# Where the output gates' weights are written, whose room the third merge gate takes, and where two splits stand on ScalarE

## The chip, the core and the metric

The kernel runs on one core of a Trainium2 chip. The core has several engines, each with a queue of its own that it works through in order: PE (TensorE, matrix products), ACT (ScalarE), DVE (VectorE), POOL (GpSimd) and SP (SyncE, which here issues most DMAs). They wait for each other through semaphores. The metric is the device time of one execution in microseconds (us). Three runs of the kernel before took 936.44, 936.89 and 935.8 us, a median of 936.44.

## What is computed

One layer of a hybrid decoder in float32, over 512 positions with 16 meta tokens ahead of them and a model width of 1024. A forgetting-attention branch and an mLSTM branch share the normalised input; two sigmoid gates merge them.

```
h = rms_norm(x, g_pre);  z = h @ w_in
(fq, fk, fv, ff, fz, mqk, mv, mi, mf, mo, mz, ga, gb) = jnp.split(z, SPLIT_POINTS, axis=-1)

oa = forgetting_attention(fq, fk, fv, log_sigmoid(ff + b_fox_f))      # 8 heads of 128, causal, blocks of 128
ya = (oa * jax.nn.silu(fz)) @ w_a

qk = jax.nn.silu(causal_conv(mqk, conv_w, conv_b));  mq, mk = jnp.split(qk, 2, axis=-1)
hb = mlstm_scan(mq, mk, mv, mi + b_i, log_sigmoid(mf + b_f))          # 4 heads, chunks of 128
hb = jax.nn.sigmoid(mo) * hb
hb = rms_norm(hb, g_head)                                             # per head
yb = (hb * jax.nn.silu(mz)) @ w_b

merged = jax.nn.sigmoid(ga) * ya + jax.nn.sigmoid(gb) * yb
return x + rms_norm(merged @ w_o, g_post)
```

`mo` is the output gate of the mLSTM heads, `mz` its silu gate, `ga` and `gb` are the merge gates, `fq` the queries of the attention.

## The kernel before

**Arithmetic.** Every float32 operand of a product is split in two: a high part in the type fp32r (a copy by ACT, name ending in `_h`) and the remainder (a subtraction by DVE, name ending in `_l`). One product is then three matmuls (`mm3`, L149 to L152). Weights arrive raw by DMA (`_r`), are split, and then read by PE.

**Seven products instead of eight.** Most projections multiply 2x2 blocks by the scheme of Strassen and Winograd. `st_products` runs seven block products in the order X, Y, Z, W, Y, X, Z. Some results must be kept aside in between, in a tile called `snap`: ACT copies it after the second product (L318), after the fourth (L323) and after the sixth (L328), and DVE joins the parts at the end (L331, L332, L334). The copy of L318 must be over before PE may write the fifth product into the same bank. The weights of the products are letters: `a` (a11), then sums. `st_narrow` (256 columns) makes a, b, c, d; `st_wide` (512 columns) makes a to g. Its sums are DVE additions in the raw tiles (L281, L282, L287, L289 in `st_wide`; L261, L262, L267, L268 in `st_narrow`), each followed by splits.

**Stages.** For each of four mLSTM heads h: convolution, values, scores (`score_part`: products, times decay L766, split L767, L769, and for the meta tokens L771), output gate (`mo_part`, wide, weights `wo{h}`, banks `po`, snap `so`), values times scores (`value_part`, banks `pna`, `pnb`), silu gates (`mz_part`, narrow, weights `wz{h}0`, `wz{h}1`). In the tile names an index of the head stands behind the letters: wo1c is letter c of head 1's output gate, wz10b letter b of its first silu unit. After the heads come attention queries (`fq_part`, snap `fqs`), keys (`fk_part`), merge gates (`ga_part`, `gb_part`, through `gate_part`, snap and result `sga`, `sgb`), the attention itself (probabilities `pth`, `ptl`, products `pfo`), and at the end the output products `pya`, `pout`. `ga_part` stores its result to DRAM (`d_sa`, L982, on ACT's DMA queue).

**What sets the order.** A scheduler orders the instructions of each engine by the order in which the program writes them and by what they depend on. Tiles are taken from pools under a tag; a new tile of a tag waits until the old one's last reader is done. The raw weights rotate through four rooms, so do `whi` and `wlo`; the tags `w` (decay weights of the scores, then `so`, later `fqs`), `sg` (merge gates) and `big_l` (remainders of transposed rows or probabilities) have one room each. Where the program wants an order without a dependency it uses `behind(x, y)` (L369): x is put behind y in the schedule, with no semaphore.

## Time and profile before

| | |
|---|---|
| median of three runs | 936.44 us |
| profiled execution | 936.34 us |
| its span, first to last instruction | 934.5 us |
| mean granted TensorE clock | 0.996 |

The time between the span and the execution, 1.8 us, lies outside the instructions. Rows of the profile read so: in a timeline, start in us, duration, engine, line, operation, output <- inputs, shape, and in brackets how long the engine had been idle and what ended that. In a view of waits: engine, tile and line that waited, `<-` what it waited for, then total us, number of waits and the longest. In a windows row: the stretch, its length, then for each engine its busy time and instructions, the clock, the DMA share and GB/s.

### The profile page before, as it was taken

The numbers are of one execution on the slowest core, as the hardware profiler recorded it, in microseconds if no ns is written. First come the engines' busy times: TensorE is split into PE (matmuls) and PEld (weight loads), VectorE is DVE, ScalarE is ACT, GpSimd is POOL, SyncE is SP. The second block draws the span as 40 slices with busy tenths as digits, with TensorE's granted clock in tenths as the row PEclk, the third lists the DMA queues.
The fourth block names the chain that finished last, engine by engine and source line by source line (L and its number), as shares of the span: only waits on it lengthen the run. The fifth ranks groups of instructions, "written<-read, shape, count | busy, mean of one in ns | idle before, by whom it ended". The sixth has DMA issues, their size and how long they took to land. (4 is left out here: it accounts for less than half of the span.)

```text
span 934.5 us, 16333 instructions
## 1 busy us (share of the span) xinstructions
PE 909.3 (97%) x6568; PEld 854.5 (91%) x6568; DVE 709.9 (76%) x1168; ACT 491.3 (53%) x840; POOL 110.0 (12%) x168
## 2 busy tenths in 40 slices
PE   8999999999999999999999999999999999999997
PEld 6998899899998999989899979899998999998887
DVE  6889688589787698876988856588885687995534
ACT  5646556546565455663565425455763554863231
POOL 3052000100101000010000002121331121300000
PEclk9999999999999999999999999999999999999999
DMA  7213143123331333232233344224352224358402
GB/s 231 93 49 102 46 134 93 34 68 94 122 103 57 90 91 92 97 96 72 71 114 92 101 125 138 73 75 136 95 190 75 75 69 137 97 190 306 136 23 91
DMA packets 76614, 97.51 MB, mean 104 GB/s; under 512 B 5237, under 2 KB 62677, under 8 KB 76538
## 3 DMA queue, kind: packets, MB, share of 16 engines
q1 hardware_dynamic: 74472, 92.76, 32.3%
q0 software_dynamic: 576, 2.10, 0.6%
q10 hardware_dynamic: 1490, 1.61, 0.5%
q8 instruction: 51, 0.84, 0.4%
q14 instruction: 25, 0.20, 0.1%
HBM read 90.62 MB, written 5.83 MB: 103 GB/s over the span
## 5 line engine op out<-in xcount | busy, mean ns | idle before, releaser
L151 PE MATMUL pyb<-bl,wb_h 128*128 128x512 f32 x128 | 49.9, 389 | 0.0
L152 PE MATMUL pyb<-bh,wb_l 128*128 128x512 f32 x128 | 49.8, 389 | 0.0
L150 PE MATMUL pyb<-bh,wb_h 128*128 128x512 f32 x128 | 49.8, 389 | 0.0
L1019 POOL TENSOR_SCALAR pn<-lt,rsum 128x128 f32<-128x128 f32 x32 | 29.3, 917 | 131.5 <-DVE rsum L1017 96.0
L733 DVE SCALAR_TENSOR_TENSOR y<-z,gc,y 128x512 f32<-128x512 f32 (+1 forms) x48 | 36.0, 756 | 2.1 <-ACT y L726 1.4
L150 PE MATMUL pfk<-hh,wfk_h 128*128 128x264 f32 x128 | 36.4, 285 | 0.0
L150 PE MATMUL pqk<-hh,wq_h 128*128 128x258 f32 x128 | 36.4, 284 | 0.0
L150 PE MATMUL pqk<-hh,wk_h 128*128 128x264 f32 x128 | 36.3, 284 | 0.0
L151 PE MATMUL pfk<-hl,wfk_h 128*128 128x264 f32 x128 | 36.3, 284 | 0.0
L152 PE MATMUL pqk<-hh,wk_l 128*128 128x264 f32 x128 | 36.3, 284 | 0.0
L152 PE MATMUL pfk<-hh,wfk_l 128*128 128x264 f32 x128 | 36.3, 283 | 0.0
L151 PE MATMUL pqk<-hl,wk_h 128*128 128x264 f32 x128 | 36.3, 283 | 0.0
L152 PE MATMUL pqk<-hh,wq_l 128*128 128x258 f32 x128 | 36.1, 282 | 0.0
L151 PE MATMUL pqk<-hl,wq_h 128*128 128x258 f32 x128 | 36.0, 282 | 0.0
L849 POOL TENSOR_TENSOR mrs<-mss,mhalf 128x1 f32<-128x1 f32 x16 | 12.2, 760 | 195.4 <-DVE r L836 157.1
L152 PEld LDWEIGHTS pyb<-bh,wb_l 128*128 128x128 f32 x128 | 24.0, 188 | 4.9
L151 PEld LDWEIGHTS pyb<-bl,wb_h 128*128 128x128 f32 x128 | 24.0, 188 | 4.9
L150 PEld LDWEIGHTS pyb<-bh,wb_h 128*128 128x128 f32 x128 | 24.0, 188 | 4.9
L144 DVE TENSOR_TENSOR wo_l<-wo_r,wo_h 128x1024 fp32r<-128x1024 f32 x12 | 15.7, 1314 | 16.9 <-ACT wo_h L142 16.9
L1016 ACT ACTIVATE lt<-lt,mn 128x144 f32<-128x144 f32 (+3 forms) x32 | 18.3, 572 | 17.9 <-DVE mn L1011 17.9
L884 DVE TENSOR_TENSOR yb<-pyb,yb 128x512 f32<-128x512 f32 x24 | 16.5, 687 | 14.2 <-PE pyb L152 14.2
L142 ACT ACTIVATE wo_h<-wo_r 128x1024 fp32r<-128x1024 f32 x12 | 12.7, 1059 | 24.4 <-PE pya L151 13.2
(2062 smaller groups left out, 3870.5 us busy)
## 6 DMA issues: line engine op xcount, KB each, us to landing
wv_r<-in_w_in_dram SPq DMA_DIRECT2D x16, 512.0 KB, 4.1
wo_r<-in_w_in_dram SPq DMA_DIRECT2D x16, 512.0 KB, 3.7
wz_r<-in_w_in_dram SPq DMA_DIRECT2D x16, 512.0 KB, 3.8
wb_r<-in_w_b_dram SPq DMA_DIRECT2D x16, 512.0 KB, 3.6
ab<-d_na SPq DMA_DIRECT2D x8, 672.0 KB, 3.9
wq_r<-in_w_in_dram SPq DMA_DIRECT2D x8, 512.0 KB, 3.8
wk_r<-in_w_in_dram SPq DMA_DIRECT2D x8, 512.0 KB, 4.4
wfq_r<-in_w_in_dram SPq DMA_DIRECT2D x8, 512.0 KB, 3.8
```

Of the source, the lines that this page charges most:

```text
L142: pin(S.activation(hi, raw, AF.Copy))
L144: pin(V.tensor_tensor(lo, raw, f(hi), ALU.subtract))
L150: T.matmul(ps, ah, bh, start=start, stop=False, **kw)
L151: T.matmul(ps, ah, bl, start=False, stop=False, **kw)
L152: T.matmul(ps, al, bh, start=False, stop=stop, **kw)
L733: V.scalar_tensor_tensor(y[:, t0:L], z[:, m, t0 + j:L + j], gc[:, j * 16 + mi:j * 16 + mi + 1], y[:, t0:L], ALU.mult, ALU.add)
L849: G.tensor_tensor(rs, ss, mhalf, ALU.pow)
L884: V.tensor_tensor(dst, ps[i], dst, ALU.add)
L1016: S.activation(lt[:, 0:kn], lt[:, 0:kn], AF.Exp, bias=mn[:, li:li + 1], scale=-1.0, accum_out=rsum)
L1019: G.tensor_scalar(pn[:, o:o + P].rearrange("p (g t) -> p g t", g=4), lt[:, 0:32].unsqueeze(1).to_broadcast([P, 4, 32]), rsum, None, ALU.mult)
```

## The change

Four edits; the work is the same, only its order and one room differ.

1. For heads 1 to 3 the output gate's `st_wide` (its loads, sums and splits) is written ahead of `score_part`, and its result passed to `mo_part`.
2. In `fq_part(0)` the last sum and the last split of the weights are put behind the last additions and the last sigmoid of the silu gate before (`mz_part.late`).
3. In `gb_part(0)` the first split is put behind the last snap copy of `ga_part(0)`.
4. `ga_part(2)` takes the room `big_l` of the pool `wk` instead of `sg`.

```diff
@@ -253,11 +253,13 @@
         split.first = first
         return hi, lo
 
-    def st_narrow(c0, name, into=None, late=None):
+    def st_narrow(c0, name, into=None, late=None, first=None):
 
         (r0,), (r1,) = (wload(win, 512 * i, 4, c0, 256, f"{name}{i}")[0] for i in range(2))
         a, b = slice(0, P), slice(P, 2 * P)
         o = {"a11": split(r0[:, :, a], f"{name}a", ("whs", "wls"), mw, 1, into)}
+        if first:
+            behind(split.first, first)
         V.tensor_tensor(r0[:, :, a], r0[:, :, a], r0[:, :, b], ALU.add)
         V.tensor_tensor(r0[:, :, b], r0[:, :, b], r1[:, :, b], ALU.add)
         x, y = split(r0, f"{name}b")
@@ -325,7 +327,7 @@
         between(1)
         prod("X", "s2", "t2")
         for wz, yx, snap, _ in units:
-            S.activation(snap[:, 2], yx[:, 256:512], AF.Copy)
+            st_products.copied = S.activation(snap[:, 2], yx[:, 256:512], AF.Copy)
         prod("Z", "s4", "b22")
         for wz, yx, snap, _ in units:
             V.tensor_tensor(yx[:, 256:512], snap[:, 0], yx[:, 256:512], ALU.subtract)
@@ -780,13 +782,13 @@
             S.activation(so[:, b, :], pn[b], AF.Sigmoid)
         return so
 
-    def mo_part(h):
+    def mo_part(h, w):
         so = sb([P, NCH, MV], F32, "w", f"so{h}")
         pn = banks(f"po{h}", NCH)
 
         snaps = [so.rearrange("p s (m n) -> p m s n", m=2)[:, m] for m in range(2)]
         units = [(pn[m], pn[2 + m], snaps[m], slice(m * P, m * P + P)) for m in range(2)]
-        added = st_products(st_wide(C_MO + h * MV, f"wo{h}"), units)
+        added = st_products(w, units)
 
         dry = line(wk, f"dry{h}", 1, tag="ss", bufs=8)
         pin(S.activation(dry, mhalf, AF.Sigmoid))
@@ -797,10 +799,11 @@
         mo_part.late = late
         return so
 
-    def st_unit(c0, name, room, into=None, late=None):
+    def st_unit(c0, name, room, into=None, late=None, first=None):
 
         ps = banks(f"p{name}", 2)
-        st_products(st_narrow(c0, f"w{name}", into, late), [(ps[0], ps[1], room.rearrange("p a (b n) -> p (a b) n", b=2), None)])
+        st_unit.added = st_products(st_narrow(c0, f"w{name}", into, late, first),
+                                    [(ps[0], ps[1], room.rearrange("p a (b n) -> p (a b) n", b=2), None)])
         return ps
 
     def mz_part(h, u):
@@ -811,7 +814,7 @@
             into = t[:, 0], t[:, 1]
         ps = st_unit(C_MZ + h * MV + u * 256, f"z{h}{u}", g, into, mo_part.late if h and not u else None)
         for m in range(2):
-            S.activation(g[:, m, :], ps[m], AF.Sigmoid)
+            mz_part.late = st_unit.added, S.activation(g[:, m, :], ps[m], AF.Sigmoid)
         for m in range(2):
             mi = 80 + h * 4 + u * 2 + m
             V.scalar_tensor_tensor(g[:, m, :], ps[m], gc[:, mi:mi + 1], g[:, m, :], ALU.mult, ALU.mult)
@@ -912,8 +915,9 @@
             next(tokens, None)
             wpk = score_part(h, q, k, w)
         else:
+            wo_ = st_wide(C_MO + h * MV, f"wo{h}")
             wpk = score_part(h, q, k, w)
-            so = mo_part(h)
+            so = mo_part(h, wo_)
         hts, gz = [None] * NCH, []
         value_part(h, wpk, v, so, hts, (3, 2))
         gz.append(mz_part(h, 0))
@@ -923,7 +927,8 @@
 
 
     def fq_part(p):
-        ps = st_unit(C_FQ + p * 256, f"fq{p}", sb([P, 2, SEQ], F32, "w", f"fqs{p}"))
+        ps = st_unit(C_FQ + p * 256, f"fq{p}", sb([P, 2, SEQ], F32, "w", f"fqs{p}"),
+                     late=None if p else mz_part.late)
         s = -(FD ** -0.5)
         qh = sb([P, 2, SEQ], F32R, "qk0h", f"fqh{p}")
         ql = sb([P, 2, SEQ], F32R, "qk0l", f"fql{p}")
@@ -964,22 +969,23 @@
             S.activation(sz[:, m, :], ps[m], AF.Sigmoid)
             V.tensor_tensor(sz[:, m, :], ps[m], sz[:, m, :], ALU.mult)
 
-    def gate_part(c0, u, name):
-        sg = sb([P, 2, SEQ], F32, "sg", f"s{name}{u}", gp)
-        ps = st_unit(c0 + u * 256, f"{name}{u}", sg)
+    def gate_part(c0, u, name, first=None, room=("sg", gp)):
+        sg = sb([P, 2, SEQ], F32, room[0], f"s{name}{u}", room[1])
+        ps = st_unit(c0 + u * 256, f"{name}{u}", sg, first=first)
         for m in range(2):
             S.activation(sg[:, m, :], ps[m], AF.Sigmoid)
         return sg
 
     def gb_part(u):
 
-        sg = gate_part(C_GB, u, "gb")
+        sg = gate_part(C_GB, u, "gb", None if u else ga_part.copied)
         y = yb[:, 2 * u:2 * u + 2, :]
         G.tensor_tensor(y, y, sg, ALU.mult)
         nc.gpsimd.dma_start(d_yb[u], y)
 
     def ga_part(u):
-        nc.scalar.dma_start(d_sa[u], gate_part(C_GA, u, "ga"))
+        nc.scalar.dma_start(d_sa[u], gate_part(C_GA, u, "ga", room=("big_l", wk) if u == 2 else ("sg", gp)))
+        ga_part.copied = st_products.copied
 
     def prob_part(p, m, q, k):
 
```

All line numbers from the second edit on shift, by 2 in most of what follows (L318 becomes L320, L328 becomes L330, L766 becomes L768, L771 becomes L773), and by 5 or 6 near the end.

The first place is DVE in head 1, from the decay of the scores on (`w`, `wl`, `wh`: score weights; `wo1b_l` and so on: remainders of the output gate's weights). Before:

```order
L769 TENSOR_TENSOR wl_2310<-w_1874,wh_2309 128x512
L769 TENSOR_TENSOR wl_2310<-w_1874,wh_2309 128x384
L769 TENSOR_TENSOR wl_2310<-w_1874,wh_2309 128x256
L766 TENSOR_TENSOR w_1874<-ps_2341,w_1874 128x128
L766 TENSOR_TENSOR w_1874<-ps_2351,w_1874 128x512
L769 TENSOR_TENSOR wl_2310<-w_1874,wh_2309 128x128
L282 TENSOR_TENSOR wo_r_2368<-wo_r_2368,wo_r_2372 128x1024
L771 TENSOR_TENSOR wh_2309<-w_1874,wh_2309 32x512
L252 TENSOR_TENSOR wo1b_l<-wo_r_2366,wo1b_h 128x1024
L252 TENSOR_TENSOR wo1c_l<-wo_r_2368,wo1c_h 128x1024
L252 TENSOR_TENSOR wo1d_l<-wo_r_2370,wo1d_h 128x1024
L252 TENSOR_TENSOR wo1e_l<-wo_r_2372,wo1e_h 128x1024
```

After, from the second sum on:

```order
L284 TENSOR_TENSOR wo_r_2306<-wo_r_2306,wo_r_2310 128x1024
L252 TENSOR_TENSOR wo1b_l<-wo_r_2304,wo1b_h 128x1024
L768 TENSOR_TENSOR w_1874<-ps_2351,w_1874 128x512
L252 TENSOR_TENSOR wo1c_l<-wo_r_2306,wo1c_h 128x1024
L252 TENSOR_TENSOR wo1d_l<-wo_r_2308,wo1d_h 128x1024
L771 TENSOR_TENSOR wl_2350<-w_1874,wh_2349 128x512
L768 TENSOR_TENSOR w_1874<-ps_2361,w_1874 128x384
L252 TENSOR_TENSOR wo1e_l<-wo_r_2310,wo1e_h 128x1024
L771 TENSOR_TENSOR wl_2350<-w_1874,wh_2349 128x384
L289 TENSOR_TENSOR wo_r_2310<-wo_r_2304,wo_r_2310 128x1024
L768 TENSOR_TENSOR w_1874<-ps_2371,w_1874 128x256
L291 TENSOR_TENSOR wo_r_2308<-wo_r_2308,wo_r_2310 128x1024
```

and right behind these:

```order
L252 TENSOR_TENSOR wo1f_l<-wo_r_2310,wo1f_h 128x1024
L771 TENSOR_TENSOR wl_2350<-w_1874,wh_2349 128x256
L252 TENSOR_TENSOR wo1g_l<-wo_r_2308,wo1g_h 128x1024
L768 TENSOR_TENSOR w_1874<-ps_2381,w_1874 128x128
L768 TENSOR_TENSOR w_1874<-ps_2391,w_1874 128x512
L771 TENSOR_TENSOR wl_2350<-w_1874,wh_2349 128x128
L252 TENSOR_TENSOR wz10a_l<-wz_r_2672,wz10a_h 128x512
L773 TENSOR_TENSOR wh_2349<-w_1874,wh_2349 32x512
```

Sum L282 (now L284) and the remainders b, c, d have moved ahead of most of the score weights; the last of these, L771 (now L773), has moved from ahead of b to behind g. On ACT at the same place the splits c to g, the copies of `so` and the first silu weights stood so before:

```order
L250 ACTIVATE wo1c_h<-wo_r_2368 128x1024
L250 ACTIVATE wo1d_h<-wo_r_2370 128x1024
L250 ACTIVATE wo1e_h<-wo_r_2372 128x1024
L318 ACTIVATE so_2361<-po_2_2364 128x2x256
L318 ACTIVATE so_2361<-po_3_2365 128x2x256
L250 ACTIVATE wz10a_h<-wz_r_2672 128x512
L250 ACTIVATE wo1f_h<-wo_r_2372 128x1024
L250 ACTIVATE wo1g_h<-wo_r_2370 128x1024
L323 ACTIVATE so_2361<-po_0_2362 128x256
L323 ACTIVATE so_2361<-po_1_2363 128x256
L250 ACTIVATE wz10b_h<-wz_r_2672 128x1024
L250 ACTIVATE wz11a<-wz_r_2847 128x512
```

and stand so after:

```order
L250 ACTIVATE wz10a_h<-wz_r_2672 128x512
L250 ACTIVATE wo1f_h<-wo_r_2310 128x1024
L769 ACTIVATE wh_2349<-w_1874 128x256
L250 ACTIVATE wo1g_h<-wo_r_2308 128x1024
L769 ACTIVATE wh_2349<-w_1874 128x128
L769 ACTIVATE wh_2349<-w_1874 128x512
L250 ACTIVATE wz11a<-wz_r_2847 128x512
L320 ACTIVATE so_2401<-po_2_2404 128x2x256
L320 ACTIVATE so_2401<-po_3_2405 128x2x256
L325 ACTIVATE so_2401<-po_0_2402 128x256
L325 ACTIVATE so_2401<-po_1_2403 128x256
L250 ACTIVATE wz10b_h<-wz_r_2672 128x1024
```

The copies of `so` have moved behind g, behind the score weights and behind the split wz11a.

The second place is ACT at the first attention query unit (`gz`: silu gate of head 3, `fqs`: snap of the unit). Before:

```order
L323 ACTIVATE gz_5681<-pz_0_5683 128x256
L250 ACTIVATE wfq0d_h<-wfq_r_5813 128x1024
L328 ACTIVATE gz_5681<-pz_1_5684 128x256
L142 ACTIVATE wfk_h_5977<-wfk_r_5973 128x1024
L250 ACTIVATE wga0a_h<-wga_r_6098 128x512
L814 ACTIVATE gz_5681<-pz_0_5683 128x512
L814 ACTIVATE gz_5681<-pz_1_5684 128x512
L318 ACTIVATE fqs_5808<-pfq_1_5810 128x512
```

After:

```order
L325 ACTIVATE gz_5681<-pz_0_5683 128x256
L330 ACTIVATE gz_5681<-pz_1_5684 128x256
L817 ACTIVATE gz_5681<-pz_0_5683 128x512
L817 ACTIVATE gz_5681<-pz_1_5684 128x512
L320 ACTIVATE fqs_5808<-pfq_1_5810 128x512
L250 ACTIVATE wfq0d_h<-wfq_r_5813 128x1024
L142 ACTIVATE wfk_h_5977<-wfk_r_5973 128x1024
L142 ACTIVATE wfk_h_5981<-wfk_r_5975 128x1024
```

The split wfq0d_h has moved from ahead of the gate's copy and sigmoids to behind them and behind the unit's first copy. A few rows on, at the first merge gate, ACT had wgb0a_h ahead of two copies of `sga`:

```order
L142 ACTIVATE wb_h_6223<-wb_r_6217 128x1024
L250 ACTIVATE wgb0a_h<-wgb_r_6354 128x512
L323 ACTIVATE sga_6095<-pga_0_6096 128x256
L142 ACTIVATE wb_h_6287<-wb_r_6283 128x1024
L328 ACTIVATE sga_6095<-pga_1_6097 128x256
```

and has it behind them:

```order
L142 ACTIVATE wb_h_6223<-wb_r_6217 128x1024
L325 ACTIVATE sga_6095<-pga_0_6096 128x256
L142 ACTIVATE wb_h_6287<-wb_r_6283 128x1024
L330 ACTIVATE sga_6095<-pga_1_6097 128x256
L250 ACTIVATE wgb0a_h<-wgb_r_6354 128x512
```

The third place is the third merge gate (`sga_9295`, weights `wga2`), on PE. Before, the fifth product (t4 times wga2c) follows the fourth (hh times wga2c):

```order
L150 MATMUL pga_0_9296<-hh,wga2c_h 128x256
L151 MATMUL pga_0_9296<-hl,wga2c_h 128x256
L152 MATMUL pga_0_9296<-hh,wga2c_l 128x256
L150 MATMUL pga_1_9297<-t4h,wga2c_h 128x256
L151 MATMUL pga_1_9297<-t4l,wga2c_h 128x256
L152 MATMUL pga_1_9297<-t4h,wga2c_l 128x256
```

After, the last attention products (`pfo`) and the beginning of the fourth merge gate (`wga3`) stand in between; here their end:

```order
L1067 MATMUL pfo_9426<-pth_9265,fvh_8097 128x128
L1068 MATMUL pfo_9426<-ptl_9266,fvh_8097 128x128
L1069 MATMUL pfo_9426<-pth_9265,fvl_8098 128x128
L1070 MATMUL pfo_9426<-ptm_9267,fvm_8099 128x512
L150 MATMUL pga_1_9446<-hh,wga3a_h 128x256
L151 MATMUL pga_1_9446<-hl,wga3a_h 128x256
L150 MATMUL pga_1_9297<-t4h,wga2c_h 128x256
L151 MATMUL pga_1_9297<-t4l,wga2c_h 128x256
L152 MATMUL pga_1_9297<-t4h,wga2c_l 128x256
```

On ACT the next rows before are:

```order
L318 ACTIVATE sga_9295<-pga_1_9297 128x512
L1074 ACTIVATE g_9423<-yb 128x1024
L323 ACTIVATE sga_9295<-pga_0_9296 128x256
L250 ACTIVATE wga3a_h<-wga_r_9447 128x512
L328 ACTIVATE sga_9295<-pga_1_9297 128x256
L250 ACTIVATE wga3b_h<-wga_r_9447 128x1024
L250 ACTIVATE wga3c_h<-wga_r_9449 128x1024
L971 ACTIVATE sga_9295<-pga_0_9296 128x512
L971 ACTIVATE sga_9295<-pga_1_9297 128x512
L982 DMA d_sa_5807<-sga_9295 128x1024
L1074 ACTIVATE g_9441<-yb 128x1024
```

and after:

```order
L1080 ACTIVATE g_9423<-yb 128x1024
L250 ACTIVATE wga3a_h<-wga_r_9447 128x512
L320 ACTIVATE sga_9295<-pga_1_9297 128x512
L325 ACTIVATE sga_9295<-pga_0_9296 128x256
L1080 ACTIVATE g_9441<-yb 128x1024
L250 ACTIVATE wga3b_h<-wga_r_9447 128x1024
L250 ACTIVATE wga3c_h<-wga_r_9449 128x1024
L330 ACTIVATE sga_9295<-pga_1_9297 128x256
L976 ACTIVATE sga_9295<-pga_0_9296 128x512
L976 ACTIVATE sga_9295<-pga_1_9297 128x512
L987 DMA d_sa_5807<-sga_9295 128x1024
L320 ACTIVATE sga_9444<-pga_1_9446 128x512
```

The unit's copies L318 and L328 have moved back, the latter behind the split of the last normalised rows (`g_9441`) and two splits of the next gate.

## The prediction

> **What bounds the kernel now.** I read the page's summary first.
>
> ```profile
> span 934.5 us, 16333 instructions
> PE 909.3 (97%) x6568; PEld 854.5 (91%) x6568; DVE 709.9 (76%) x1168; ACT 491.3 (53%) x840; POOL 110.0 (12%) x168
> PEclk9999999999999999999999999999999999999999
> wz_r<-in_w_in_dram SPq DMA_DIRECT2D x16, 512.0 KB, 3.8
> ```
>
> TensorE (PE) is busy for 97% of the span, at full clock in every slice. The change adds and removes no instruction, so only PE's pauses can move the time. Next I read the view of waits, which says for each pause of PE what ended it.
>
> ```profile
> PE po L150 <- ACT wo3c_h L250: 2.1, 1, 2.1
> PE pfq L150 <- ACT fqs L318: 2.0, 3, 1.0
> PE pga L150 <- ACT sga L318: 1.6, 1, 1.6
> PE po L150 <- ACT wo2c_h L250: 1.5, 1, 1.5
> PE po L150 <- ACT wo1c_h L250: 1.5, 1, 1.5
> PE pga L150 <- ACT sga L323: 1.5, 1, 1.5
> ```
>
> Each of the four edits aims at some of these: the output gates' weights at the wo1c, wo2c and wo3c rows, the third merge gate's room at sga L318, the two ordered splits at sga L323 and at one of the three fqs pauses, the longest. Together 2.1 + 1.0 + 1.6 + 1.5 + 1.5 + 1.5 = 9.2 us. A pause costs more than its idle time. The end of a matmul is modelled 0.28 us after its start, while the next may start 0.12 us after it, which adds 0.16; and the first matmuls after a pause come about 0.11 us late. So idle plus 0.27 each, **10.8 us** for all six. That is the most the change can win directly; the question is what stands behind each pause.
>
> **Output gates (three times).** Rows of the stage for head 1, from the timelines of PE, ACT (ScalarE) and DVE (VectorE), one windows row for the DVE work of the stage, and one row of head 3.
>
> ```profile
> 207.59 0.28 PE L150 MATMUL po<-wo1a_h,hh 128*128 128x256 f32 x1
> 210.47 0.39 PE L150 MATMUL po<-wo1b_h,t3h 128*128 128x256 f32 x2
> 212.37 0.51 PE L150 MATMUL po<-wo1c_h,t1h 128*128 128x256 f32 x2 [1.52 <-ACT wo1c_h L250]
> ...
> 211.26 1.06 ACT L250 ACTIVATE wo1c_h<-wo_r 128x1024 fp32r<-128x1024 f32 x1 [0.76 <-DVE wo_r L282]
> 224.72 0.63 ACT L250 ACTIVATE wz11a<-wz_r 128x512 fp32r<-128x512 f32 x1
> ...
> 206.16 1.48 DVE L766 TENSOR_TENSOR w<-ps,w 128x512 f32<-128x512 f32 x3
> 208.95 0.89 DVE L766 TENSOR_TENSOR w<-ps,w 128x128 f32<-128x128 f32 x2
> 209.94 1.23 DVE L282 TENSOR_TENSOR wo_r<-wo_r,wo_r 128x1024 f32<-128x1024 f32 x1
> 211.20 0.69 DVE L771 TENSOR_TENSOR wh<-w,wh 32x512 fp32r<-32x512 f32 x1
> 220.93 1.22 DVE L252 TENSOR_TENSOR wo1g_l<-wo_r,wo1g_h 128x1024 fp32r<-128x1024 f32 x1
> ...
> 206.16:222.15 15.99, 14.47 (x115) 13.99 (x115) 15.74 (x22) 9.64 (x15) 0.00 (x0) 1.00 0.24 67
> ...
> 474.35 0.63 ACT L250 ACTIVATE wz31a<-wz_r 128x512 fp32r<-128x512 f32 x1 [1.02 <-DMA wz_r<-in_w_in_dram]
> ```
>
> The chain now: sum L282 waits behind the score weights' work on DVE until 209.94, ACT splits wo1c_h until 212.3, and PE restarts at 212.37. 24 starts from 207.59 to 210.47 give 0.12 us a matmul. The windows row shows that DVE is full here: 15.74 of 15.99 us. So the change can't shorten the DVE work, it only deals it out anew. In the order after, L282 and the splits of b, c and d come early, and the score weights' four multiplications (L766) and remainders (L769, L771) are strung out between e, f and g.
>
> I add up the DVE rows in that order from 206.2. Rows in sequence overlap by 0.09 us, so 1024 columns take 1.23 - 0.09 = 1.14 and 512 take 0.69 - 0.09 = 0.60; the three L766 (512, 384 and 256 columns) take 1.48 - 0.09 = 1.39 together, which I part into 0.60, 0.46 and 0.33, and the two at 208.95 (128 and 512) leave 0.20 for 128. Sum done 207.4, wo1c_h at 208.5, wo1c_l at 210.3. PE, with no pause, needs c at 207.59 + 48 x 0.12 = 213.3. **The pause at c goes.** But f_l ends at 217.9, g_l at 219.4 and L771, the last of the score weights, only at 221.6, where it ended at 211.9 before.
>
> Who waits for L771 now? PE's last value products of these weights, and ACT's copies of `so`, since that tile takes the room of the weights that L771 reads. Product e may start only when the copies (L318) are done. ACT has them behind the split wz11a, which waits for its load; and this is issued when f_l leaves its buffer. By the page's median of 3.8 us it lands at 217.9 + 3.8 = 221.7; split (0.57) and copy (0.60) end near 222.8. PE, now running a, b, c, d and 23 value products ahead of e, gets there at about 221.7 by itself, so **a new pause of about 1 us stands at e**. The same 119 matmuls were done before at 212.37 + 93 x 0.118 + 0.2 = 223.55. Gain: 223.55 - 222.8 = 0.75 us. Head 3's load took longer: ACT idled 1.02 us for it until 474.35, which I put at 4.6 us from its issue; I take 0.5 there. **Sum 2.0 us.** Bounds per head: +1.9 (no pause at e), -1.0 (the load lands 1.7 us later, about 5.5). I take the middle since both chains, by L771 and by the load, end near 222.
>
> **First query unit of the attention.** Rows of ACT, DVE and PE.
>
> ```profile
> 507.60 1.06 ACT L250 ACTIVATE wfq0d_h<-wfq_r 128x1024 fp32r<-128x1024 f32 x1 [3.35 <-DVE wfq_r L268]
> 512.05 0.59 ACT L318 ACTIVATE fqs<-pfq 128x512 f32<-128x512 f32 x1
> ...
> 506.42 0.49 DVE L850 TENSOR_SCALAR ht<-ht,mrs 128x512 f32<-128x512 f32 x1 [0.44 <-POOL mrs L849]
> 506.82 0.69 DVE L268 TENSOR_TENSOR wfq_r<-wfq_r 128x512 f32<-128x512 f32 x1
> 512.50 1.41 DVE L817 SCALAR_TENSOR_TENSOR gz<-pz,gc,gz 128x512 f32<-128x512 f32 x2
> ...
> 510.09 0.28 PE L150 MATMUL pfq<-hh,wfq0c_h 128*128 128x256 f32 x1
> 512.69 0.38 PE L150 MATMUL pfq<-t4h,wfq0c_h 128*128 128x256 f32 x1 [1.01 <-ACT fqs L318]
> ```
>
> ACT sat 3.35 us before wfq0d_h, and everything up to the fqs copy queued behind it. After, the gate's copy, its sigmoids and fqs stand ahead of that split, so fqs ends near 510.3, before PE wants it (12 products after 510.09, 511.5). The pause of 1.0 (1.27 with restart) goes. But L268 now comes behind the gate's last three adds (256, 512 and 512 columns, 1.6 us by the spacings above) and its two L817 (1.41 us): adds from 506.9, the end of L850, to 508.5, L267 to 509.1, L817 to 510.6, L268 to 511.3; split (1.06) to 512.4, remainder (1.23) to 513.7. PE wants d at 510.09 + 24 x 0.117 = 512.9: **a new pause of 0.75, with restart 0.85**. Net **+0.4 us**, from 0 to 1.27.
>
> **First merge gate.**
>
> ```profile
> 534.58 1.06 ACT L142 ACTIVATE wb_h<-wb_r 128x1024 fp32r<-128x1024 f32 x1 [0.70 <-PE pga L151]
> 539.33 0.63 ACT L250 ACTIVATE wgb0a_h<-wgb_r 128x512 fp32r<-128x512 f32 x1 [3.69 <-DMA wgb_r<-in_w_in_dram]
> 539.87 0.36 ACT L323 ACTIVATE sga<-pga 128x256 f32<-128x256 f32 x1
> ...
> 540.28 0.38 PE L150 MATMUL pga<-hh,wga0d_h 128*128 128x256 f32 x1 [1.52 <-ACT sga L323]
> ```
>
> ACT stood 3.69 us for a load in front of a copy that PE wanted. After, copy L323 comes right behind wb_h, over 2 us before PE needs it; the late split has gone behind copy L328, and its first user is a unit later. Cover is long, so the whole pause is won: **1.8 us** (1.5 to 1.8).
>
> **Third merge gate.**
>
> ```profile
> 822.94 0.60 ACT L318 ACTIVATE sga<-pga 128x512 f32<-128x512 f32 x1 [0.80 <-DMA d_sa<-sga]
> ...
> 823.59 0.39 PE L150 MATMUL pga<-t4h,wga2c_h 128*128 128x256 f32 x1 [1.56 <-ACT sga L318]
> 827.85 0.40 PE L1061 MATMUL pfo<-pth,fvh 128*128 128x512 f32 x1
> 829.99 0.28 PE L150 MATMUL pga<-hh,wga3a_h 128*128 128x256 f32 x1
> 836.99 0.28 PE L150 MATMUL pga<-t2h,wga3d_h 128*128 128x256 f32 x1
> 839.77 0.40 PE L150 MATMUL pya<-gh,wa_h 128*128 128x512 f32 x1
> ...
> 834.91 1.23 DVE L252 TENSOR_TENSOR wga3d_l<-wga_r,wga3d_h 128x1024 fp32r<-128x1024 f32 x1
> ```
>
> The copy waits for the store of the gate before, whose room it shares. In the new room lie the remainders of the last probabilities, which the last attention products (pfo) read. The order has moved these from behind the unit to the place of the pause: 13 products of 2.1 us in all (827.85 to 829.99). They end near 824.2, the copy at 824.9, so PE waits about 0.7 instead of 1.8 and would be 1 us ahead: next gate's d at 836.0 to 836.2 instead of 836.99. It doesn't keep this. On ACT the split of the last normalised rows (to 828.3), wga3b_h (829.3) and wga3c_h (830.3) now stand ahead of the unit's copy L328 (830.7), and the unit's three adds on DVE behind that copy (832.3). Then come wga3c_l (833.4), the two sums (834.7), wga3d_h (835.8) and wga3d_l (837.1), which PE wants at 836.2: a new pause of 0.9. Output products pya would start at 839.8, as before. Net **0** (-0.5 to +1.8).
>
> **Sum.** 2.0 + 0.4 + 1.8 + 0 = 4.2 us. The profiled execution took 936.34 us (the span and 1.8 around it), 0.1 under the median of the runs shown, so about **932.1 us**.
>
> **A rule of the skill.** No pause of PE above exceeds 2.1 us and the granted clock is full throughout. The Trainium skill, page "TensorE: Matmul & The Clock Gate", section "HAM oscillation — how this bites in real kernels", warns of PE idle gaps above about 3.4 us, after which the clock is throttled; the trace agrees in that none here is so long and no slice shows a lower clock. By that rule removing these pauses wins nothing beyond their length, and a new pause at e of over 3.4 us would cost more than its length.
>
> **Rivals.**
> - *All six pauses go and nothing takes their place*: 936.34 - 10.8 = 925.5 us. For it: PE is the bound. Against: DVE is full in the stage of the output gates, and three new late operands stand in the orders. Chance 0.08.
> - *The output gates win nothing*: the wait at c simply becomes one at e (L771 or the load 0.7 us later than I have them), and the query unit and third gate are even. Only the first merge gate is left: about 934.4 us. Chance 0.22.
> - *Slower*: ACT's split wz11a, now ahead of the so copies, holds them until its load lands. With issue at 217.9, e starts at 219.1 plus the landing time; break-even for a head is 4.5 us. With 2.2 us won elsewhere, the whole change breaks even at 5.2 us. At 6.0 us each head loses 1.5: 936.34 + 4.5 - 2.2 = 938.6 us. Against it: median 3.8 us and 4.6 in head 3. Chance 0.05.
> - *The third gate's copy doesn't wait less*, if the new room comes free later than I have it: 0.5 us worse than forecast, within its range.
>
> **Chances.** My forecast, between 929 and 934, has 0.65. The range, 928.5 to 935.0, takes in the second rival and leaves out the first, the slower one and a few hundredths for a better mix. A difference under 0.2% (1.9 us) can't be told from no change here: faster by more 0.80, within 0.15, slower by more 0.05.
>
> **What would show it.** In the view of waits after: no row for wo1c, wo2c, wo3c and none for sga L323 (steps one and three right). New rows for PE at product e, ended by so L318 (now with a shifted line number) or by the last weights' remainder, near 1 us each; if they are absent the gates win up to 1.9 each, if over 1.9 they lose. For the query unit a pause at wfq0d_l or wfq0d_h near 0.7; for the third gate one of 0.5 at its copy and one near 0.9 at wga3d_l. I am wrong if the loads of wz land much earlier or later than 3.8 us, if DVE's order leaves it idle in the stage, or if time won at these places is lost at a later wait that I didn't follow.

## The result and the profile after

The changed kernel takes **931.06 us** (median of four runs, 930.5 to 931.39) where the kernel before takes 936.12 us (four runs, 935.26 to 936.89). The ratio is 0.9946, with a 95% interval of 0.9928 to 0.9963. The forecast was 932.1 us, in a range of 928.5 to 935.0.

The page's summary of the changed kernel, and then its view of waits for PE, down to waits of 0.4 us:

```profile
span 929.5 us, 16316 instructions
PE 910.4 (98%) x6568; PEld 854.1 (92%) x6568; DVE 710.0 (76%) x1168; ACT 492.4 (53%) x840; POOL 110.0 (12%) x168
```

```profile
PE pnb L832 <- ACT wh L769: 1.7, 3, 0.7
...
PE pfq L150 <- ACT fqs L320: 1.1, 2, 0.5
PE pnb L835 <- DVE wh L773: 1.0, 3, 0.4
...
PE pga L152 <- DVE wga3d_l L252: 0.7, 1, 0.7
...
PE pl L150 <- DVE ptl L1053: 0.4, 1, 0.4
PE pga L152 <- DVE wga3b_l L252: 0.4, 1, 0.4
```

All six rows that the change aimed at are gone: no wo1c, wo2c, wo3c, no copy of `sga`, and the `fqs` group has two waits instead of three. New are the three waits for L773 (the last of the score weights, one per head), a third wait for L769 (the split of the score weights on ACT), and the waits for wga3b_l, wga3d_l and a `ptl`. The group of L769 was this before, both of its waits in head 0; the third one now is in head 3:

```profile
PE pnb L829 <- ACT wh L767: 1.3, 2, 0.7
```

PE's busy time hardly moved (909.3 to 910.4 us), so the 5 us are idle time.

A pause on PE delays everything behind it, so the start of one and the same matmul in both timelines shows what was won up to there. This table is worked out from the first matmul of the named weights in the two profiles.

| first matmul of | before | after | difference | step, won in it |
|---|---|---|---|---|
| a score product of head 1 (the third of 384 columns) | 204.14 | 203.42 | -0.72 | ahead of the edits |
| wz10a (output gate of head 1 done) | 234.91 | 233.40 | -1.50 | 0.78 |
| wz20a (head 2) | 359.01 | 356.91 | -2.10 | 0.60 |
| wz30a (head 3) | 483.81 | 480.98 | -2.82 | 0.73 |
| wfq0c (query unit) | 510.09 | 507.32 | -2.77 | |
| wfq0d | 514.17 | 510.13 | -4.04 | 1.27 |
| wgb0a (first merge gate done) | 563.61 | 557.77 | -5.84 | 1.80 |
| wfq3a (attention) | 763.77 | 757.66 | -6.10 | 0.26 |
| wga2c (third merge gate) | 820.45 | 815.22 | -5.24 | -0.86 |
| wa (output products) | 839.77 | 834.75 | -5.02 | -0.22 |

The 0.72 us at the top are hardly the change's: the kernels below that have only the second, third or fourth edit, whose PE order is that of the kernel before, stood 0.5 to 1.0 us ahead of its profile at that product too. The loss of 0.86 us before the third merge gate isn't its doing either. The DVE timelines before and after show it:

```profile
776.45 0.69 DVE L262 TENSOR_TENSOR wfz_r<-wfz_r,wfz_r 128x512 f32<-128x512 f32 x1 [2.20 <-DMA wfz_r<-in_w_in_dram]
```

```profile
771.38 0.69 DVE L264 TENSOR_TENSOR wfz_r<-wfz_r,wfz_r 128x512 f32<-128x512 f32 x1 [3.18 <-DMA wfz_r<-in_w_in_dram]
```

The sum waits for a load in both, 1.0 us longer in this profile; in eight other profiles with the same edits or none in this stretch it stood between 0.4 won and 0.8 lost against before. What is lost goes with the load. In the three profiles in which this sum waited 2.8 us or more (this one, the third edit alone, and the second of the two runs of the second edit alone) the stretch lost 0.7 to 0.9 us, and PE waited 0.35 to 0.56 us for `ptl`; in the others the sum waited 2.4 us or less, and none of them has a wait for `ptl`.

### The profile page after: what moved, and what is told of

It is laid out like the page before. It is cut to its first block, busy times and chain, and to the rows that moved or that the text cites. A ratio compares the mean times of both kernels' runs of the same rounds, so it can differ in the third digit from the quotient of the medians.

```text
span 929.5 us, 16316 instructions
## 1 busy us (share of the span) xinstructions
PE 910.4 (98%) x6568; PEld 854.1 (92%) x6568; DVE 710.0 (76%) x1168; ACT 492.4 (53%) x840; POOL 110.0 (12%) x168
## 4 chain that ended last, share of the span: by engine, by line
PE 72%; DVE 17%; ACT 5%; issue 3%; DMA 1%; POOL 1%; DVEq 0%; POOLq 0%; ACTq 0%
PE pyb L150 3%; PE pyb L151 3%; PE pyb L152 3%; PE pz L150 3%; PE pz L151 3%; PE pz L152 3%; PE pqk L150 3%; PE pqk L152 3%; PE pqk L151 3%; PE pv L150 2%; PE pv L152 2%; PE pv L151 2%; PE pfk L150 2%; PE pfk L152 2%; PE pfk L151 2%
## 5 line engine op out<-in xcount | busy, mean ns | idle before, releaser
L852 POOL TENSOR_TENSOR mrs<-mss,mhalf 128x1 f32<-128x1 f32 x16 | 9.2, 576 | 191.4 <-DVE mss L850 188.1
L1002 POOL TENSOR_TENSOR ab<-ab,mask_q 128x128 f32<-128x128 f32 x32 | 21.0, 684 | 49.0 <-DMA ab<-d_na 49.0
```

What stands on the lines that cost most here:

```text
L852: G.tensor_tensor(rs, ss, mhalf, ALU.pow)
L1002: G.tensor_tensor(ab[:, o:o + P], ab[:, o:o + P], mask_q, ALU.add)
```

## Each edit alone

Four kernels have one edit each. The difference from the changed kernel is that the other three are undone:

```diff
 # first edit undone
-            wo_ = st_wide(C_MO + h * MV, f"wo{h}")
             wpk = score_part(h, q, k, w)
-            so = mo_part(h, wo_)
+            so = mo_part(h, st_wide(C_MO + h * MV, f"wo{h}"))
 # second
-        ps = st_unit(C_FQ + p * 256, f"fq{p}", sb([P, 2, SEQ], F32, "w", f"fqs{p}"),
-                     late=None if p else mz_part.late)
+        ps = st_unit(C_FQ + p * 256, f"fq{p}", sb([P, 2, SEQ], F32, "w", f"fqs{p}"))
 # third
-        sg = gate_part(C_GB, u, "gb", None if u else ga_part.copied)
+        sg = gate_part(C_GB, u, "gb")
 # fourth
-        nc.scalar.dma_start(d_sa[u], gate_part(C_GA, u, "ga", room=("big_l", wk) if u == 2 else ("sg", gp)))
+        nc.scalar.dma_start(d_sa[u], gate_part(C_GA, u, "ga"))
```

The first edit alone:

> Only the first edit (output gates' weights written ahead of the scores), the other three undone. Theory (each edit acts in its own stage, the time won is the sum): the pauses at wo1c, wo2c and wo3c are gone, about 0.7 us is won in each head's output gate against the kernel before, as in the changed kernel (0.78, 0.60, 0.73), and 0.3 us in head 0, whose value products are ordered otherwise too: 936.1 - 2.4 = 933.7 us. The new pauses at the meta-token product (ended by L773, about 0.5 us) and at product e (ended by the so copy, 0.2 to 0.3 us) are there in all three heads. Rival (the edits depend on each other; the gates alone win nothing once the silu gates wait as before): 936 us, with the 0.7 us per head lost again ahead of the attention.

The second:

> Only the second edit (last sum and split of the first query unit's weights behind the silu gate's last adds and sigmoid). My step in the prediction: the pause at the fqs copy goes (1.27 us) but a new one of 0.75 to 0.85 us stands at product d, since sum L268 comes only behind the gate's two L817; net 0.4, so 935.7 us. Rival, from the changed kernel's trace (no pause at d there): the silu gate's last adds come early enough and 1.27 us are won in full, 934.8 us. If the changed kernel was saved at d only by the first edit, which lets the DVE rows ahead run earlier, the new pause is seen here.

The third:

> Only the third edit (first split of the fifth narrow unit behind the last snap copy of the first merge gate). Theory: the pause at wga0d is gone and nothing else moves: 1.8 us from there to the end, 934.3 us. Rival: part of it is lost again at the split that now comes later or at a load in the attention: less than 1.2 us at the end.

The fourth:

> Only the fourth edit (other room for the third merge gate). Theory: the pause of 1.6 us idle at its fifth product shrinks, and pauses at wga3b_l (about 0.4 idle) and wga3d_l (about 0.7) stand in its place, net within 0.3 us of nothing: 936.1 us. Rival (the two new pauses come from the time won earlier, not from the order): 1.8 us won, 934.3 us.

Measured, with what each profile shows in the stages (worked out as in the table above):

| edit alone | time, us | ratio to before | output gates of heads 1 to 3 | query unit | first merge gate | third merge gate |
|---|---|---|---|---|---|---|
| first | 932.4 | 0.9954 (0.9937 to 0.9972) | 0.80, 0.42, 0.72 | 1.27 | 0.44 | 0.0 |
| second | 933.92 | 0.9968 (0.9958 to 0.9978) | 0.22, -0.21, -1.21 | 1.27 | 1.79 | 0.0 |
| third | 935.0 | 0.9981 (0.9968 to 0.9994) | 0.01, 0.01, 0.48 | -0.05 | 1.79 | -0.1 |
| fourth | 935.87 | 0.999 (0.9979 to 1.0) | 0.40, 0.02, 0.21 | -0.10 | 0.10 | -0.2 |
| all four | 931.06 | 0.9946 (0.9928 to 0.9963) | 0.78, 0.60, 0.73 | 1.27 | 1.80 | -0.2 |

Stages without an edit differ by up to 0.5 us between single profiles; the -1.21 is a fall of the clock, told in the last section. The gains don't add up: 4.3 + 3.0 + 1.8 + 0.9 is 10 us by the ratios, and together they win 5.1. **Two pauses are each removed by two edits**, so 1.27 + 1.79 = 3.1 us are counted twice; the other 1.8 us of the difference are no more than the four intervals allow. The pause at the query unit goes with the first edit alone and with the second alone. The pause at the first merge gate goes with the third alone and with the second alone: there the order put the split wgb0a_h behind one more copy by itself. In ACT's timeline of the second edit alone the copy stands ahead of the split that waits 2.82 us for its load:

```profile
534.99 0.38 ACT L325 ACTIVATE sga<-pga 128x256 f32<-128x256 f32 x1 [0.43 <-PE pga L152]
538.19 0.63 ACT L250 ACTIVATE wgb0a_h<-wgb_r 128x512 fp32r<-128x512 f32 x1 [2.82 <-DMA wgb_r<-in_w_in_dram]
```

The first edit won more than I expected of it alone (933.7 us), since it also takes the query unit's pause. So did the second (935.7 us, or 934.8 by its rival), since it also takes the first merge gate's. The third won what its theory said by the ratio, 1.8 us, with an interval of 0.6 to 3.0. In its one profile 1.5 us of that were lost again to two late loads in the attention: 0.75 to that of the table above, and 0.7 to one that the split wfz1a waits for, told below. The fourth wins nothing in its own stage, as expected: -0.2 us, and its interval reaches to 1.0.

To see whether the second edit adds anything beside the first, it alone was taken out of the changed kernel:

> The changed kernel without its second edit. In the run of the first edit alone the pause at the fqs copy was already gone, as in the run of the second alone. Theory: the two edits win the same 1.27 us, so the second adds nothing here: 931.1 us, as the changed kernel, no pause at product c of the query unit. Rival (in the run of the first edit alone this was chance, for instance of a load): the pause of about 1 us is back and the time is 932.3 us.

It took 931.77 us (ratio 0.9954, 0.9938 to 0.9969), which can't be told from the changed kernel. In its profile 1.27 us are won at wfq0d and 1.79 at the first merge gate, as with all four edits. The theory held: given the first and the third edit, the second adds nothing. But its view of waits has the row

```profile
PE pfq L150 <- ACT fqs L320: 2.1, 2, 1.5
```

and that is another query unit, the second. Its ACT timeline shows a split ahead of the copy, waiting for a load:

```profile
631.73 0.63 ACT L250 ACTIVATE wfz1a_h<-wfz_r 128x512 fp32r<-128x512 f32 x1 [0.89 <-DMA wfz_r<-in_w_in_dram]
632.26 0.58 ACT L320 ACTIVATE fqs<-pfq 128x512 f32<-128x512 f32 x1
```

In the changed kernel's profile the same split didn't wait, and the pause there was 0.5 us. Twelve profiles have this order. In eight of them the split didn't wait and PE's pause was 0.5 us; in four it waited 0.7 to 1.0 us for the load, and the pause was 1.3 to 1.6 us. So how late one load lands can make about 1 us of the scatter from run to run.

## What stands behind the output gates' pause

The changed kernel in head 1, from the timelines of PE, ACT and DVE:

```profile
220.91 0.38 PE L835 MATMUL pnb<-vm,wh 112*128 112x258 f32 x1 [0.34 <-DVE wh L773]
222.02 0.39 PE L150 MATMUL po<-wo1e_h,t4h 128*128 128x256 f32 x1
...
220.85 0.63 ACT L250 ACTIVATE wz11a<-wz_r 128x512 fp32r<-128x512 f32 x1 [0.85 <-DMA wz_r<-in_w_in_dram]
221.39 1.07 ACT L320 ACTIVATE so<-po 128x512 f32<-128x512 f32 x2
...
217.32 1.22 DVE L252 TENSOR_TENSOR wo1g_l<-wo_r,wo1g_h 128x1024 fp32r<-128x1024 f32 x1
220.17 0.69 DVE L773 TENSOR_TENSOR wh<-w,wh 32x512 fp32r<-32x512 f32 x1
```

Two pauses have taken the place of one. The meta-token product waits for L773, which ends behind g at 220.86: from start to start 0.50 us more than the usual 0.12. Product e waits for the copy of `so`, which stands behind the split wz11a and its load, 0.29 us more. Around them five starts come 0.1 us late. Head 3 has a third pause, of 0.45 us idle, at a value product that waits for one of the last splits of the score weights (L769). That split waits for its multiplication L768, which stands behind g on DVE as L773 does:

```profile
466.80 0.39 PE L832 MATMUL pnb<-vh,wh 128*128 128x258 f32 x1 [0.45 <-ACT wh L769]
```

All late starts of this stage added up (steps from start to start of over 0.15 us, less the usual 0.12) cost PE 1.9, 1.9 and 2.4 us in heads 1 to 3 before, and 1.3, 1.3 and 1.9 us after. Two kernels take one cause each.

The first puts only the split wz11a behind the copies of `so`:

```diff
-            S.activation(snap[:, 0:2], halves(yx), AF.Copy)
+            st_products.kept = S.activation(snap[:, 0:2], halves(yx), AF.Copy)
...
         added = st_products(w, units)
+        mo_part.kept = st_products.kept
...
-    ps = st_unit(C_MZ + h * MV + u * 256, f"z{h}{u}", g, into, mo_part.late if h and not u else None)
+    ps = st_unit(C_MZ + h * MV + u * 256, f"z{h}{u}", g, into, mo_part.late if h and not u else None,
+                 mo_part.kept if h and u else None)
```

> The changed kernel, but the first split of the second silu unit is put behind the so copies on ACT, so that these don't stand behind a load. Theory: product e no longer waits (0.2 to 0.3 us and a restart of 0.1 a head), the pause at the meta-token product (0.5) stays, since it hangs on DVE alone: 931.1 - 1.1 = 930.0 us. Rival: the so copies end no earlier, because they wait for L773 (room of the score weights) as well, and e waits as before: 931.1 us.

It took 930.2 us (0.9933, 0.9915 to 0.9951), as expected, and the three heads won 1.14, 0.94 and 1.04 us where the changed kernel won 0.78, 0.60 and 0.73. Its PE timeline has the wait for L773 still, and none at e:

```profile
220.63 0.38 PE L837 MATMUL pnb<-vm,wh 112*128 112x258 f32 x1 [0.34 <-DVE wh L773]
221.33 0.32 PE L150 MATMUL po<-wo1e_h,t4h 128*128 128x256 f32 x1
```

So the load ahead of the copies did hold e, and the late score weights were the rest.

The second writes the sums and splits of f and g behind the scores, and only a to e ahead of them:

```diff
-        V.tensor_tensor(a22, a11, a22, ALU.add)
-        o["s2"] = split(a22, f"{name}f")
-        V.tensor_tensor(a12, a12, a22, ALU.add)
-        o["s4"] = split(a12, f"{name}g")
-        return o
+        def rest():
+            V.tensor_tensor(a22, a11, a22, ALU.add)
+            o["s2"] = split(a22, f"{name}f")
+            V.tensor_tensor(a12, a12, a22, ALU.add)
+            o["s4"] = split(a12, f"{name}g")
+            return o
...
-            wo_ = st_wide(C_MO + h * MV, f"wo{h}")
+            wo_ = st_wide(C_MO + h * MV, f"wo{h}", True)
             wpk = score_part(h, q, k, w)
+            st_wide.rest()
```

> The changed kernel, but the last two sums and splits (f and g) of each output gate's weights are written behind the scores, the rest ahead of them as in the change. Theory: the new pauses at the meta-token value product (0.5 us) and at product e (0.2 to 0.3 us) come from the score weights ending behind f and g on DVE; with these behind, L773's counterpart ends about 3.5 us earlier, both pauses go in all three heads and with the slow restarts 0.9 to 1.2 us a head are won: about 928 us. Rival 1: product e waits for the split of the silu weights that stands ahead of the so copies on ACT, whatever DVE does: only the pause at the meta-token product goes, about 929.5 us. Rival 2: f or g now comes too late for PE and the pause moves there: 931 us.

It took **926.41 us** (0.9897, 0.9881 to 0.9912), some 4.6 us less than the changed kernel, more than expected. Its DVE timeline, and then the one row of `po` that is left in its view of waits:

```profile
215.94 0.69 DVE L779 TENSOR_TENSOR wh<-w,wh 32x512 fp32r<-32x512 f32 x1
217.81 1.22 DVE L252 TENSOR_TENSOR wo1f_l<-wo_r,wo1f_h 128x1024 fp32r<-128x1024 f32 x1
```

```profile
PE po L150 <- ACT so L326: 0.2, 1, 0.2
```

The last of the score weights (now L779) ends at 216.6 instead of 220.9, no value product waits for it, and e starts at 217.86 instead of 222.02. The copies of `so` came ahead of wz11a by themselves. The heads win 2.34, 1.79 and 2.16 us, about the whole of the old pauses. The expectation had counted 0.9 to 1.2 us a head in the changed kernel; the late starts there are 1.3, 1.3 and 1.9 us, head 3's third pause among them, and of these 0.0, 0.15 and 0.5 are left. This settles it: DVE is full in this stage (busy for 15.94 of 16.0 us from the second sum on, in the changed kernel and in this one), so it matters which of its work PE needs first, and in the changed kernel f and g, needed last, stood ahead of the score weights.

## The third merge gate

> The changed kernel, but the third merge gate takes a room that has been free for 30 us by then (that of the attention's decay rows) instead of that of the last probabilities' remainders. Theory: its copy waits for nothing, the order of PE there is that of the kernel before (the last attention products behind the unit), none of the pauses at the unit's fifth product, at wga3b_l and at wga3d_l is left, and 1.8 us are won against the kernel before in this stage instead of 0.2 lost: 929.0 us. Rival (the new pauses at wga3b_l and wga3d_l come from the time won at the copy, whichever room it has): pauses of 0.4 and 0.7 are seen at these splits, and the time is 930.5 us.

The edit is one word, the room of the attention's decay rows:

```diff
-gate_part(C_GA, u, "ga", room=("big_l", wk) if u == 2 else ("sg", gp))
+gate_part(C_GA, u, "ga", room=("ab", gp) if u == 2 else ("sg", gp))
```

It took 929.78 us (0.9934, 0.9918 to 0.995). In its stage 0.92 us are won where the changed kernel loses 0.22; the waits for wga3b_l and wga3d_l are gone. The expected 1.8 were halved by a pause of 0.65 us at the same copy, which ACT's and PE's timelines explain:

```profile
815.29 1.06 ACT L250 ACTIVATE wga2d_h<-wga_r 128x1024 fp32r<-128x1024 f32 x1 [0.85 <-DVE wga_r L270]
816.25 0.58 ACT L320 ACTIVATE sga<-pga 128x512 f32<-128x512 f32 x1
...
816.88 0.39 PE L150 MATMUL pga<-t4h,wga2c_h 128*128 128x256 f32 x1 [0.65 <-ACT sga L320]
```

The room is free, and now the copy stands behind a split that waits for DVE, once more the pattern of the second and third edit.

Both new edits together, and then three more splits put behind the copies that PE waits for (the last of this unit, and the first ones of two silu units, wfz1a and wfz3a, behind the query units' copies):

> Two of the edits that won, together: f and g of the output gates behind the scores, and the third merge gate in the decay rows' room. Theory: they act in different stages and add up: 926.4 - 1.2 = 925.2 us, with one pause of 0.6 us left at the third merge gate's fifth product, ended by its copy, which stands behind a split that waits for VectorE's sum. Rival: the time won at the end of the output gates is lost to loads in the attention: 926.4 us.

> As the kernel with both edits, and three more splits are put behind the copy for which TensorE waits, as the change does for two: the last split of the third merge gate's weights behind that unit's first copy, and the first split of the second and the fourth silu unit of the attention (wfz1a, wfz3a) behind the first copy of the query unit ahead. Theory: the pause of 0.6 us at the third merge gate and the pauses of 0.5 us (1.5 in some runs, when the load of wfz1 lands late) at the second and fourth query unit are gone, 2 to 3 us: 922.5 us. Rival: the splits themselves come too late then, and the pauses move to wga2d or wfz a: 925 us.

The core of the three orders:

```diff
+        fq_part.kept = st_products.kept
...
-        ps = st_unit(C_FZ + p * 256, f"fz{p}", sz)
+        ps = st_unit(C_FZ + p * 256, f"fz{p}", sz, first=fq_part.kept if p % 2 else None)
...
+            if own:
+                behind(split.first, st_products.kept)
```

The two edits together took 926.52 us (0.9891, 0.9876 to 0.9905), so the room's gain can't be told in the time beside the other (0.6 us by the ratios, within the intervals), though its profile has it in the stage (0.81 us): its expectation of 925.2 was missed. With the three orders it is **924.85 us** (0.9874, 0.9857 to 0.989), the fastest kernel of the study, where 922.5 was expected and 925 by the rival. Its view of waits has no `fqs` row any more, but a new one

```profile
PE pga L152 <- DVE wga2d_l L252: 0.5, 1, 0.5
```

so at the third merge gate the pause moved to the split, as the rival said, and at the query units it is gone, as the theory said.

## Why the prediction was right, and where not

- **Bound.** PE's idle time decided. That holds: 5 us won with PE's busy time unchanged.
- **Output gates.** Predicted 0.75, 0.75 and 0.5, 2.0 in all; measured 0.78, 0.60 and 0.73, 2.1. The mechanism (DVE full, L773 late, the copies behind wz11a) is shown by the two kernels that take one cause each. The times in head 1 came out too: moved by the 0.72 us that PE was ahead, L773 ended at 221.6, wz11a started at 221.6 and e at 222.7, where I had 221.6, 221.7 (the load's landing) and 222.8. But I put one pause of about 1 us at e; it is two, 0.50 at the meta-token product and 0.2 to 0.3 at e, with slow restarts, and a third in head 3. I had named the value products as waiting for L771 (now L773) and then priced only the copy.
- **Query unit.** Predicted 0.4, measured 1.27; this step failed. I carried the times of DVE's rows ahead of the gate's last adds over from before and let only the order behind them change. "Adds from 506.9" is 504.1 when moved by the 2.77 us that PE was ahead there; they began at 502.3, and so the last sum and split ended in time:

```profile
495.19 1.23 DVE L252 TENSOR_TENSOR wz31d_l<-wz_r,wz31d_h 128x1024 fp32r<-128x1024 f32 x1 [1.19 <-ACT wz31d_h L250]
```

```profile
492.59 1.22 DVE L252 TENSOR_TENSOR wz31d_l<-wz_r,wz31d_h 128x1024 fp32r<-128x1024 f32 x1
...
502.32 0.43 DVE L333 TENSOR_TENSOR pz<-gz,pz 128x256 f32<-128x256 f32 x1 [0.15 <-ACT gz L330]
507.95 1.23 DVE L252 TENSOR_TENSOR wfq0d_l<-wfq_r,wfq0d_h 128x1024 fp32r<-128x1024 f32 x1 [1.13 <-ACT wfq0d_h L250]
```

  The first of these rows is of before, the others of after. Before, DVE idled 1.19 us in front of wz31d_l with the adds of the unit ahead still to do. After, the first edit's new order has those adds in front of it and the idle time is filled. Of the 1.8 us by which the adds came early, 1.5 are there at wfq0c_l already (504.03 before, 499.74 after, less the 2.77). The rest goes with the sum L267. Where it stands between L847 and L850 (before, and with the first edit alone) these two start 1.25 us apart; where it stands behind the adds (after, and with the second alone) 0.8 us. I moved it behind the adds and left its time in "506.9" as well. The chain behind the adds took 6.9 us, as I had it (6.8). PE started d at 510.13, and wfq0d_l ended at 509.2. With the first edit alone DVE has no idle time in front of wz31d_l either; with the second alone it is still there:

```profile
494.31 1.23 DVE L252 TENSOR_TENSOR wz31d_l<-wz_r,wz31d_h 128x1024 fp32r<-128x1024 f32 x1 [1.18 <-ACT wz31d_h L250]
```

  So the first edit fills it. That this is what took the new pause away was read from the traces and not tried by itself. Whether the second edit alone would leave a pause at d is open, since in both its profiles the clock fell ahead of it (below).
- **First merge gate.** Predicted 1.8, measured 1.80, and alone 1.79. I didn't see that the second edit's order removes this pause too.
- **Third merge gate.** Predicted 0, measured -0.2. The pause at wga3d_l (0.7 idle, 0.8 from start to start) is as named, but that the sum came out is luck in part, since two errors cancel. I had PE wait about 0.7 us for the copy, until the last of the 13 attention products was done. It waited 0.2 from start to start (0.06 idle): the copy waited only for the last product that reads `ptl` (L1068), two products before the last of the 13, and two products of wga3a filled in. About as much, 0.5, went to a pause at wga3b_l, which I had inside the chain only.

```profile
818.78 0.60 ACT L320 ACTIVATE sga<-pga 128x512 f32<-128x512 f32 x1 [0.39 <-PE pfo L1068]
```

- **Sum.** Predicted 4.2, measured 5.1 by the medians. Of the profiles' 5.0 us the four stages hold 4.95 (2.1 + 1.27 + 1.80 - 0.22); the 0.72 and 0.26 ahead and between them pay for the 0.86 of the late load. The query unit is what the forecast missed.

## What to carry to other kernels

When one engine is the bound, list its pauses and ask for each what is late next: here six pauses of 10.8 us gave 5. At the output gates 2.1 of 5.9 us were won, since the same full engine had to deliver something else first; at the third merge gate nothing, since other operands came late next. In an in-order queue, look for an instruction that waits for a load or a slow sum in front of a short copy on which the bound engine depends; that pattern made the pauses at the first query unit and the first merge gate before, and new ones at e and in the decay rows' room after. Edits to an order reach beyond their place, so undo each alone: the second edit's two gains each come with another edit too (the first, the third), and beside those two it added nothing that could be told.

## What the runs showed of the hardware

The prediction said that the clock was full throughout. The page's 40 slices show a 9 each (90% or more), but a slice is 23 us long. In stretches of 2 us the kernel before has a fall to half speed ahead of head 1, less than 2 us behind three pauses of 0.55, 0.70 and 0.70 us idle (PE restarts at 100.99, 102.19 and 103.27):

```profile
102.00:104.00 2.00, 1.03 (x4) 0.62 (x5) 1.88 (x6) 1.03 (x3) 0.00 (x0) 1.00 0.36 128
104.00:106.00 2.00, 2.00 (x14) 2.00 (x14) 1.24 (x4) 0.63 (x1) 0.00 (x0) 0.75 0.00 0
106.00:108.00 2.00, 1.87 (x9) 1.57 (x9) 1.22 (x5) 0.00 (x0) 0.10 (x1) 0.50 0.00 0
```

Ten other profiles show it too, between 102 and 110 us; the profiles of the first edit alone and of the kernel with wz11a behind the copies have the three pauses and no fall. With the second edit alone a second fall follows the pause at wo3c:

```profile
460.00:462.00 2.00, 1.74 (x11) 1.69 (x12) 2.00 (x2) 2.00 (x3) 0.00 (x0) 0.82 0.02 4
462.00:464.00 2.00, 2.00 (x11) 2.00 (x11) 2.00 (x3) 0.41 (x2) 0.00 (x0) 0.50 0.30 38
```

The matmuls there start 0.21 to 0.22 us apart instead of 0.12. The kernel was run once more for this:

> The run of the second edit alone once more. In the first run the clock fell to half for 3.5 us after the pause at wo3c, so TensorE was about 1.2 us late at the query unit and the VectorE rows ahead had that much more time. Theory: the fall of the clock is chance (the kernel before has the same pause and kept its clock), and without it a pause of 0.2 to 0.4 us is seen at product d of the query unit, ended by the remainder wfq0d_l, so that the second edit alone wins about 0.9 us there. Rival: the clock falls again at the same place, and no pause is seen at d.

The rival held. The clock fell again at the same place, to 0.50, head 3 lost 1.07 us against before (1.2 in the first run), and there was no pause at d. The pause was 2.05 us idle in the first run and 1.8 in the second; the kernel before has one of 2.1 at the same place and kept its clock. So a pause of 2 us can cost its length and 1.1 to 1.2 us more.

What decides it can be read in part from the clock records. In all thirteen profiles the granted clock changes only at moments a whole multiple of 3.413 us apart: in the kernel before it was full for 92.16 us, half for 3.41 and full for 822.61, which is 27, 1 and 241 times that. Where this grid lies under the kernel differs from run to run. Five profiles have the pause at wo3c (worked out from the clock record and PE's timeline, in us):

| profile | PE idle in front of wo3c | the grid there | clock afterwards |
|---|---|---|---|
| second edit alone | 458.21 to 460.26 | whole in 457.88 to 461.29 | 0.50 |
| the same, second run | 458.48 to 460.28 | whole in 458.26 to 461.67 | 0.50 |
| kernel before | 459.22 to 461.27 | parted at 460.00 | 1.00 |
| third edit alone | 458.68 to 460.47 | parted at 459.10 | 1.00 |
| fourth edit alone | 458.09 to 460.14 | parted at 459.08 | 1.00 |

The clock fell where one stretch of 3.413 us held the whole pause, and stayed where two shared it. A pause of 1.51 us held whole (second edit alone, 209.86 to 211.37 in 208.70 to 212.11) left it full. So the fall seems to hang on how the pause meets the grid, and that the second edit's kernel met it alike twice can still be chance. This fits the five profiles; it wasn't tried by itself, and how busy a stretch must be isn't settled.

The Trainium skill, page "TensorE: Matmul & The Clock Gate", section "HAM oscillation — how this bites in real kernels", speaks of idle gaps above about 3.4 us; here the clock fell behind pauses of 2 us and less, so the measurement decides against taking that figure as a safe bound.
